# Small products of a chunk regrouped by row count on TensorE, and the decays' product on all 128 rows

## The chip, the cores and the metric

The kernel runs on one core of one Trainium2 chip. The metric is the device time of one execution in microseconds (us), as the median over runs. Matrix products run on TensorE (PE in the profile, its weight loads PEld), elementwise work on VectorE (DVE) and ScalarE (ACT), small helpers and some DMA issues on GpSimd (POOL), most loads are issued from SyncE (SP).

## The reference, cut to what matters

One decoder layer is computed for a prompt of 2048 tokens and for a small group of sample tokens. First comes a mixer with two recurrent halves, then cross-attention to 256 memory tokens, then a gated feed-forward part. The change touches the two recurrences of the prompt's mixer:

```python
def gla step(s, inp):                       # per chunk, per head, key width 64, value width 128
    qt = qc * exp(b);  kt = kc * exp(-b)
    att = where(causal, einsum('bthk,bshk->bhts', qt, kt), 0)
    o = einsum('bhts,bshv->bthv', att, vc) + einsum('bthk,bhkv->bthv', qt, s)
    s = exp(bl) * s + einsum('bshk,bshv->bhkv', kc * exp(bl - b), vc)

def ssd step(s, inp):                       # per chunk, 8 heads
    lc = cumsum(dt * a_head)
    decay = exp(where(causal, lc[t] - lc[s], -inf))
    y = (cc . bc) * decay * dt @ x  +  (cc . s) * exp(lc)
    s = exp(ll) * s + (exp(ll - lc) * dt * x) @ bc
```

The sum `o` of the first step is one product over 128 positions of the chunk (attention times values) plus one over 64 key entries (queries times state). The decays of the second step are differences of `lc`, so a row of `lc` has to be spread over 128 partitions. The kernel uses chunks of 128 tokens.

## The kernel before, in words

The prompt is handled in four blocks of 512 tokens (`block(b)`, L471), each of four chunks of 128 tokens. A block first projects its tokens (`fm`, L491, and `tm`, L628: long runs of 128-row products into banks `acc`, each row of weights times activations done as three products of the rounded parts by the helper at L125 to L129). The recurrences are cut into pieces by generators and put beside these projections through the queue `side`: SSD chunks (L709 to L778) run beside the projection `tm(1)` and those that follow it, GLA chunks (L847 to L895) of block b beside the projections of block b+1; the last block's GLA chunks run beside `folds(1)` (L424 to L468), which makes weight products for the attention stage and stores them through GpSimd's DMA queue (`wvo`). Beside blocks 0 and 1 also run, from the queue `back`, the memory keys and values, `folds(0)` and `quad_sums` (L406), whose loads and stores (`fold`, `wX`) go through GpSimd's queue too. All engines run their instructions in the written order, as the framework's scheduler has laid it down; nothing is reordered at run time apart from what an engine's own queue does.

Two places matter here.

A GLA chunk's second part (L865) makes, for each of four heads h = 2j + par, `dst = attm . v` over 128 rows (L882) and adds `q . Sp` over the 64 rows `par*64 ...` (L883). The heads of one `par` share a bank, `po[par]`. Before these stand the four products into `pS` (L875: 128 rows, 64 columns of weights), after them the next projection's products. A float32 product appears as two PE instructions in the trace, a rounded float32 (`F32R`) one as one.

An SSD chunk's first part (L709) builds `R`, 16 rows that hold the two parts of `lc` of 8 heads, masked, on GpSimd (L713), and multiplies it by ones (L739: 16 rows, 512 columns, twice), so that each of 128 partitions gets the sums. VectorE makes the decay matrix `M` from that (L743). `R` has one buffer, and shares it with a temporary of the gates (L610), which ScalarE and VectorE use earlier in the block.

Of the kernel before, what the change touches and what calls it, by code (L numbers as in the profile page):

```python
# [37 lines left out]
def f(ap):  # L38
    return ap.bitcast(F32)
# [3 lines left out]
def hymba_kernel(ctx: ExitStack, tc: tile.TileContext, a: dict, o: dict, dbg: dict | None = None):  # L43
# [427 lines left out]
    def block(b):  # L471
# [129 lines left out]
        def gates():  # L601
            pss = []
            nc.scalar.activation(sps[0:16], sp[0:16], AF.Copy)
            nc.vector.tensor_tensor(sps[32:48], sp[0:16], f(sps)[0:16], op=ALU.subtract)
            nc.scalar.activation(sps[64:80], sp[0:16], AF.Copy)
            for j in range(2):
                ps = mxt()
                nc.tensor.matmul(ps, lhsT=w2s[:, j * P:(j + 1) * P], rhs=sps, start=True, stop=True)
                pss.append(ps)
            logsig(bb[:, 0:2], pss, pa.tile([P, 2, BT], F32, name="R"), BT)  # L610
            for j in range(2):
                nc.vector.tensor_tensor_scan(bb[:, j], rmask, bb[:, j], 0.0, op0=ALU.mult, op1=ALU.add)
            b3 = bb[:, 0:2].rearrange("p j (c t) -> p (j c) t", t=CH)
            e8 = lambda t: t.rearrange("p j c -> p (j c)")
            nc.scalar.activation(e8(em), b3[:, :, 63], AF.Exp, scale=1.0 / 16)
            nc.scalar.activation(e8(ebl), b3[:, :, CH - 1], AF.Exp, scale=1.0 / 16)
            nc.vector.tensor_tensor(e8(el), b3[:, :, CH - 1], b3[:, :, 63], op=ALU.subtract)
            nc.scalar.activation(el, el, AF.Exp, scale=1.0 / 16)
            nc.vector.tensor_tensor(bb[:, 2:4].rearrange("p j (c t) -> p (j c) t", t=CH), b3, b3[:, :, 63:64].broadcast_to([P, 2 * NCH, CH]), op=ALU.subtract)
            nc.scalar.activation(bb[:, 0:2], bb[:, 2:4], AF.Exp, scale=1.0 / 16)  # L620
            nc.scalar.activation(bb[:, 2:4], bb[:, 2:4], AF.Exp, scale=-1.0 / 16)
            yield

        side.append(decays())
        step(side)
        side.appendleft(gates())
# [82 lines left out]
        def ssd_first(c):  # L709
            cs = slice(c * CH, (c + 1) * CH)  # L710

            R = pa.tile([16, 8, CH], F32R, name="R")
            nc.gpsimd.tensor_tensor(out=R, in0=lcT[:, cs].unsqueeze(1).broadcast_to([16, 8, CH]),  # L713
                                    in1=bmask.unsqueeze(2).broadcast_to([16, 8, CH]), op=ALU.mult)
            M = pa.tile([P, 8, CH], F32, name="M")

# [19 lines left out]
                                    triu.unsqueeze(1).broadcast_to([P, 2, CH]), op=ALU.mult)  # L736
            for g in range(2):
                pl = mxt()
                nc.tensor.matmul(pl, lhsT=onesr[0:16, :], rhs=R[:, 4 * g:4 * g + 4], start=True, stop=True)  # L739
                plv = pl.rearrange("p (h t) -> p h t", t=CH)  # L740
                for h in range(4):
                    s1 = lc[:, c * 8 + 4 * g + h:c * 8 + 4 * g + h + 1]
# [122 lines left out]
        def gla_second(c, am, kt_):  # L865
# [5 lines left out]
            for j in range(2):  # L871
                for par in range(2):
                    r0 = par * 64
                    h = 2 * j + par
                    nc.tensor.matmul(pS[r0:r0 + 64, j * P:(j + 1) * P], lhsT=kt_[:, h * 64:(h + 1) * 64], rhs=v[c][:, h * P:(h + 1) * P], start=True, stop=True)  # L875
            po = [mxt(), mxt()]
            for par in range(2):
                for j in range(2):
                    r0 = par * 64
                    h = 2 * j + par  # L880
                    dst = po[par][:, j * CH:(j + 1) * CH]
                    nc.tensor.matmul(dst, lhsT=am[:, 2 * par + j], rhs=v[c][:, h * P:(h + 1) * P], start=True, stop=False)  # L882
                    nc.tensor.matmul(dst, lhsT=q[r0:r0 + 64, j, cs], rhs=Sp[r0:r0 + 64, j], start=False, stop=True)  # L883
            for j in range(2):
                nc.vector.tensor_scalar(Sg[:, j], Sg[:, j], ebl[:, j, c:c + 1], None, op0=ALU.mult)
                nc.vector.scalar_tensor_tensor(Sg[:, j], pS[:, j * P:(j + 1) * P], el[:, j, c:c + 1], Sg[:, j], op0=ALU.mult, op1=ALU.add)
            ss = small.tile([P, 8], F32, name="ss")
            of = lambda h: po[h % 2][:, (h // 2) * P:(h // 2 + 1) * P]
            for h in range(4):
                nc.scalar.activation(v[c][:, h * P:(h + 1) * P], of(h), AF.Square, accum_out=ss[:, h:h + 1])  # L890
            rs = rstd_of(ss[:, 0:4], "rs", 128, cols=4)
# [1348 lines left out]
```

## Time and profile before

| | |
|---|---|
| time, median of 3 runs | 3048.89 us (3040.87 to 3052.48) |
| the profiled execution's own time | 3045.82 us |
| its span, first to last instruction | 3044.1 us |
| PE busy (matmul) | 2884.3 us, 95% |
| DVE, ACT, POOL busy | 2087.5, 1525.7, 544.3 us |
| mean granted TensorE clock | 0.977 |
| the four blocks with their recurrences | the first 914 us |

The page's times are us unless marked ns. A row of the timeline gives the start, the length, engine, line, operation, tiles, shape (rows*columns of the weights, then the moving operand) and how many instructions were merged; in brackets stands the engine's idle time before it and what ended it. Matmuls are pipelined, so a matmul's length is longer than its share of the time: the pitch from one start to the next is what it costs. The chain of waits goes back from the end, at each step to what released the instruction. A window's row gives, for each engine, busy time and instructions, then the granted TensorE clock and the DMA share.

### The profile page before, as it was taken

The numbers are of one execution on the slowest core, as the hardware profiler recorded it, in microseconds if no ns is written. First come the engines' busy times: TensorE is split into PE (matmuls) and PEld (weight loads), VectorE is DVE, ScalarE is ACT, GpSimd is POOL, SyncE is SP. The second block draws the span as 40 slices with busy tenths as digits, with TensorE's granted clock in tenths as the row PEclk, the third lists the DMA queues.
The fourth block names the chain that finished last, engine by engine and source line by source line (L and its number), as shares of the span: only waits on it lengthen the run. The fifth ranks groups of instructions, "written<-read, shape, count | busy, mean of one in ns | idle before, by whom it ended". The sixth has DMA issues, their size and how long they took to land.

```text
span 3044.1 us, 42288 instructions
## 1 busy us (share of the span) xinstructions
PE 2884.3 (95%) x15207; PEld 2408.6 (79%) x15207; DVE 2087.5 (69%) x3915; ACT 1525.7 (50%) x3044; POOL 544.3 (18%) x749
## 2 busy tenths in 40 slices
PE   8999999999997999999689999999999998999997
PEld 8887777787775778877588888888999995587875
DVE  7666676666737677677587777776678884566576
ACT  4454443554445677776554434433455553444453
POOL 2142341121321321024222100010000000011122
PEclk9999999999999999999799999999999999999998
DMA  7345543242256676467646455774243345767788
GB/s 239 118 152 161 169 125 118 70 128 75 78 187 226 242 263 227 153 202 237 195 177 212 163 172 186 258 265 160 101 150 121 119 141 183 245 139 192 158 210 246
DMA packets 154769, 529.89 MB, mean 174 GB/s; under 512 B 19360, under 2 KB 22608, under 8 KB 143040
## 3 DMA queue, kind: packets, MB, share of 16 engines
q1 hardware_dynamic: 93168, 331.75, 34.1%
q0 software_dynamic: 49152, 170.46, 18.4%
q10 hardware_dynamic: 12240, 24.99, 2.5%
q8 instruction: 120, 1.97, 0.3%
q14 instruction: 89, 0.73, 0.1%
HBM read 373.04 MB, written 154.09 MB: 173 GB/s over the span
## 4 chain that ended last, share of the span: by engine, by line
PE 57%; issue 16%; DMA 7%; DVE 6%; ACT 5%; POOL 2%; POOLq 0%; DVEq 0%; ACTq 0%; SPq 0%
PE accA L127 7%; PE accA L128 7%; PE accA L129 7%; PE accC L127 4%; PE acc L127 4%; PE acc L128 4%; PE acc L129 4%; PE accC L128 4%; PE accC L129 4%; PE accB L127 2%; PE accB L128 2%; PE accB L129 2%; PE mx L1911 1%; PE mx L1686 1%; DMA st<-wT 1%
## 5 line engine op out<-in xcount | busy, mean ns | idle before, releaser
L127 PE MATMUL accA<-r,s 128*128 128x512 f32 (+2 forms) x1792 | 645.3, 360 | 39.0 <-ACT r L1566 13.4
L129 PE MATMUL accA<-r,s 128*128 128x512 f32 (+2 forms) x1792 | 633.6, 354 | 7.1 <-DVE s L1504 6.2
L128 PE MATMUL accA<-r,s 128*128 128x512 f32 (+2 forms) x1792 | 633.9, 354 | 6.7 <-DVE r L1570 6.6
L127 PEld LDWEIGHTS accA<-r,s 128*128 128x128 f32 x1792 | 341.7, 191 | 114.7 <-ACT r L1566 17.5
L1502 ACT ACTIVATE s<-sum 128x512 fp32r<-128x512 f32 (+2 forms) x488 | 289.3, 593 | 268.4 <-DVE sum L1484 102.7
L128 PEld LDWEIGHTS accA<-r,s 128*128 128x128 f32 x1792 | 342.3, 191 | 40.8 <-DVE r L1570 12.0
L129 PEld LDWEIGHTS accA<-r,s 128*128 128x128 f32 x1792 | 341.9, 191 | 38.7 <-DVE s L1504 9.0
L127 PE MATMUL accC<-r,s 128*128 128x512 f32 (+2 forms) x896 | 325.3, 363 | 17.1 <-ACT r L1566 6.8
L1504 DVE TENSOR_TENSOR s<-sum,s 128x512 fp32r<-128x512 f32 (+2 forms) x488 | 308.8, 641 | 35.2 <-ACT s L1502 31.9
L129 PE MATMUL accC<-r,s 128*128 128x512 f32 (+2 forms) x896 | 317.9, 355 | 7.0 <-DVE s L1504 7.0
L128 PE MATMUL accC<-r,s 128*128 128x512 f32 (+2 forms) x896 | 317.6, 354 | 1.0 <-DVE r L1570 0.9
L1504 DVE TENSOR_TENSOR s<-raw,s 128x512 fp32r<-128x512 f32 (+2 forms) x366 | 234.3, 640 | 59.1 <-ACT s L1502 57.6
L1502 ACT ACTIVATE s<-raw 128x512 fp32r<-128x512 f32 (+2 forms) x366 | 218.2, 596 | 54.1 <-PE accC L129 51.3
L121 ACT ACTIVATE whi<-wraw 128x1024 fp32r<-128x1024 f32 (+2 forms) x148 | 137.1, 941 | 211.3 <-PE acc L128 107.2
L127 PEld LDWEIGHTS accC<-r,s 128*128 128x128 f32 x896 | 172.0, 192 | 61.4 <-issue 10.2
L122 DVE TENSOR_TENSOR wlo<-wraw,whi 128x1024 fp32r<-128x1024 f32 (+2 forms) x148 | 166.8, 1136 | 63.4 <-ACT whi L121 62.7
L129 PEld LDWEIGHTS accC<-r,s 128*128 128x128 f32 x896 | 171.8, 192 | 24.7 <-DVE s L1504 8.7
L1570 DVE TENSOR_TENSOR r<-st,r 128x1024 fp32r<-128x1024 f32 (+2 forms) x133 | 136.5, 1028 | 75.1 <-ACT r L1566 74.5
L128 PEld LDWEIGHTS accC<-r,s 128*128 128x128 f32 x896 | 172.0, 192 | 17.1 <-DVE r L1570 2.4
L127 PE MATMUL acc<-xh,whi 128*128 128x512 f32 (+1 forms) x464 | 170.1, 368 | 8.4 <-ACT xh L282 8.2
L129 PE MATMUL acc<-xh,wlo 128*128 128x512 f32 (+1 forms) x464 | 165.3, 358 | 1.7 <-DVE wlo L122 1.7
L128 PE MATMUL acc<-xl,whi 128*128 128x512 f32 (+1 forms) x464 | 164.7, 356 | 0.2 <-DVE xl L283 0.2
(643 smaller groups left out, 5765.0 us busy)
## 6 DMA issues: line engine op xcount, KB each, us to landing
raw<-in_w_gu_dram SPq DMA_DIRECT2D x66, 1024.0 KB, 4.9
wraw<-in_w_in_fm_dram SPq DMA_DIRECT2D x52, 512.0 KB, 3.7
wraw<-in_w_in_tm_dram SPq DMA_DIRECT2D x48, 512.0 KB, 3.7
yp<-y POOLq DMA_DIRECT2D x48, 512.0 KB, 6.9
raw<-aT SPq DMA_DIRECT2D x24, 768.0 KB, 5.3
st<-in_w_down_dram SPq DMA_DIRECT2D x34, 512.0 KB, 6.8
aT<-og POOLq DMA_DIRECT2D x22, 768.0 KB, 4.3
hX<-y POOLq DMA_DIRECT2D x32, 512.0 KB, 5.1
```

Of the source, the lines that this page charges most:

```text
L121: last[0] = nc.scalar.activation(hi[:, cs], raw[:, cs], AF.Copy)
L122: nc.vector.tensor_tensor(lo[:, cs], raw[:, cs], f(hi)[:, cs], op=ALU.subtract)
L127: nc.tensor.matmul(ps, lhsT=wh, rhs=ah, start=start, stop=False, skip_group_check=more)
L128: nc.tensor.matmul(ps, lhsT=wh, rhs=al, start=False, stop=False, skip_group_check=more)
L129: nc.tensor.matmul(ps, lhsT=wl, rhs=ah, start=False, stop=stop, skip_group_check=more)
L1502: nc.scalar.activation(h3, v, AF.Copy)
L1504: return lambda: nc.vector.tensor_tensor(l3, v, f(h3), op=ALU.subtract)
L1570: nc.vector.tensor_tensor(lo, v, f(hi), op=ALU.subtract)
L1686: nc.tensor.transpose(ps[kt // 4][:, kt % 4 * P:(kt % 4 + 1) * P], u[:, kt * P:(kt + 1) * P], ident)
L1911: nc.tensor.matmul(ps[g0:g0 + 32], lhsT=s_f[:, kt].rearrange("p h t -> p (h t)"), rhs=ws.popleft(), start=kt < 4, stop=kt >= FT - 4, tile_ ...
```

## The change

In a GLA chunk the four `attm . v` products come first, in a row, and then the four `q . Sp` products, whose heads now alternate between rows 0 to 63 and 64 to 127. Only the first `attm . v` product of each bank has the start flag. In an SSD chunk `R` becomes a tile of 128 rows, allocated once per block at the end of the gates and cleared there by GpSimd; the masked `lc` is written to rows 0 to 15 of it, and the product with ones takes all 128 rows.

```diff
@@ gates()
             nc.scalar.activation(bb[:, 2:4], bb[:, 2:4], AF.Exp, scale=-1.0 / 16)
+            Rs.append(pa.tile([P, 8, CH], F32R, name="R"))
+            nc.gpsimd.memset(f(Rs[0]), 0.0)
             yield
+        Rs = []
@@ ssd_first(c)
-            R = pa.tile([16, 8, CH], F32R, name="R")
-            nc.gpsimd.tensor_tensor(out=R, in0=lcT[:, cs].unsqueeze(1).broadcast_to([16, 8, CH]),
+            R = Rs[0]
+            nc.gpsimd.tensor_tensor(out=R[0:16], in0=lcT[:, cs].unsqueeze(1).broadcast_to([16, 8, CH]),
                                     in1=bmask.unsqueeze(2).broadcast_to([16, 8, CH]), op=ALU.mult)
...
-                nc.tensor.matmul(pl, lhsT=onesr[0:16, :], rhs=R[:, 4 * g:4 * g + 4], start=True, stop=True)
+                nc.tensor.matmul(pl, lhsT=onesr, rhs=R[:, 4 * g:4 * g + 4], start=True, stop=True)
@@ gla_second(c, am, kt_)
             po = [mxt(), mxt()]
+            of = lambda h: po[h % 2][:, (h // 2) * P:(h // 2 + 1) * P]
+
             for par in range(2):
                 for j in range(2):
-                    r0 = par * 64
                     h = 2 * j + par
-                    dst = po[par][:, j * CH:(j + 1) * CH]
-                    nc.tensor.matmul(dst, lhsT=am[:, 2 * par + j], rhs=v[c][:, h * P:(h + 1) * P], start=True, stop=False)
-                    nc.tensor.matmul(dst, lhsT=q[r0:r0 + 64, j, cs], rhs=Sp[r0:r0 + 64, j], start=False, stop=True)
+                    nc.tensor.matmul(of(h), lhsT=am[:, 2 * par + j], rhs=v[c][:, h * P:(h + 1) * P], start=j == 0, stop=False, skip_group_check=True)
+            for h in range(4):
+                r0, j = (h % 2) * 64, h // 2
+                nc.tensor.matmul(of(h), lhsT=q[r0:r0 + 64, j, cs], rhs=Sp[r0:r0 + 64, j], start=False, stop=True, skip_group_check=True)
```

On PE, in the first GLA chunk (in block 1, between `pS` and the next projection), the order before:

```order
L129 MATMUL acc<-xh_2912,wlo 128x512
L875 MATMUL mx<-v_2687,kt__2930 64x128 x4
L882 MATMUL mx<-v_2687,attm_1688 128x128
L883 MATMUL mx<-Sp,q 128x128
L882 MATMUL mx<-v_2687,attm_1688 128x128
L883 MATMUL mx<-Sp,q 128x128
```

(two more such pairs follow, then L127), and in the changed kernel, where L879 is the old L875, L886 the old L882 and L889 the old L883:

```order
L129 MATMUL acc<-xh_2910,wlo 128x512
L879 MATMUL mx<-v_2685,kt__2928 64x128 x4
L886 MATMUL mx<-v_2685,attm_1690 128x128 x4
L889 MATMUL mx<-Sp,q 128x128 x4
L127 MATMUL acc<-xh_2867,whi 128x512
L128 MATMUL acc<-xl_2868,whi 128x512
```

The eight products keep their place among PE's other work; they change places among themselves, and so do those of the other 15 chunks.

On GpSimd, at the start of block 2's SSD chunks (`carry` and `pre` belong to the convolution of the projection before them, `xw` is the SSD chunk's weighted input), the changed kernel has

```order
L534 COPY pre<-carry 128x3
L537 COPY carry<-pre 128x3
L534 COPY pre<-carry 128x3
L623 MEMSET R 128x1024
L717 TENSOR_TENSOR R<-lcT,bmask 16x1024
L729 TENSOR_TENSOR xw<-xdt,wl__5252 128x512
L717 TENSOR_TENSOR R<-lcT,bmask 16x1024
```

The clearing of `R` is the only new row there, ahead of the block's first write of `R` (before: L713); the rows around it stand as they did. The decays' products themselves (L739 before, L743 now) keep their places: this is PE around one of block 2's SSD chunks, before, and the changed kernel reads the same with the new line numbers:

```order
L733 MATMUL mx<-xc 128x128 x2
L739 MATMUL mx<-R,onesr 128x512
L127 MATMUL acc<-xh_4609,whi 128x512
L128 MATMUL acc<-xl_4610,whi 128x512
L129 MATMUL acc<-xh_4609,wlo 128x512
L739 MATMUL mx<-R,onesr 128x512
L127 MATMUL acc<-xh_4614,whi 128x512
L128 MATMUL acc<-xl_4615,whi 128x512
```

Nothing moved here: only the number of rows that L739 reads is another.

Of the 32 decays' products, 10 stand in five pairs, two in a row, and 22 stand alone among the projections' products or next to L733. Outside these places one product of `folds(1)` in the last block's tail stands a few rows earlier; nothing else moved.

More of the change, by code (lines that the diff above doesn't have):

```diff
@@ L887, in gla_second @@
             ss = small.tile([P, 8], F32, name="ss")
-            of = lambda h: po[h % 2][:, (h // 2) * P:(h // 2 + 1) * P]
             for h in range(4):
```

## The prediction

> **What bounds the kernel now.** First the page's busy times, then a table of windows over the blocks' part of the span (window and length, busy us and instructions of PE, PEld, DVE, ACT, POOL, then granted clock, DMA share, GB/s):
>
> ```profile
> PE 2884.3 (95%) x15207; PEld 2408.6 (79%) x15207; DVE 2087.5 (69%) x3915; ACT 1525.7 (50%) x3044; POOL 544.3 (18%) x749
> 130.00:302.40 172.40, 170.62 (x1010) 137.92 (x1010) 116.81 (x202) 81.55 (x156) 55.88 (x60) 1.00 0.48 150
> 302.40:387.60 85.20, 74.87 (x354) 58.19 (x352) 52.14 (x124) 42.71 (x67) 32.70 (x54) 0.98 0.50 159
> 387.60:459.00 71.40, 66.34 (x315) 53.25 (x316) 53.88 (x98) 29.88 (x58) 34.43 (x34) 0.94 0.44 129
> 459.00:866.00 407.00, 402.55 (x1951) 319.80 (x1949) 256.35 (x508) 181.90 (x338) 76.74 (x79) 0.99 0.32 95
> 873.00:904.00 31.00, 30.47 (x162) 22.28 (x162) 15.95 (x40) 17.94 (x42) 13.18 (x20) 1.00 0.65 216
> ```
>
> PE is busy nearly throughout, except in 302 to 459 (most of block 1). Busy PE is not yet the path, so the chain of waits was read window by window: the shares in 462 to 866 (blocks 2 and 3), in 302.3 to 387.7, and three long pieces of the chain.
>
> ```profile
> by line: PE acc L127 20.7%; PE acc L128 20.0%; PE acc L129 20.0%; PE mx L882 3.3%; PE mx L883 3.3%; PE mx L757 3.1%; ACT xc L198 1.8%; PE acc L516 1.8%; PE mx L767 1.8%; PE mx L694 1.8%; PE mx L754 1.7%; PE mx L739 1.6%; issue 1.6%; PE mx L
> by line: DMA fold<-in_w_out_dram 32.1%; issue 21.0%; DMA wX<-fold 17.6%; DMA wqk<-fold 6.0%; POOL fold L413 3.9%; DVE fraw L419 3.8%; DVE xc L541 3.6%; POOL wX L421 3.1%; DVE fold L419 2.9%; DVE wlo L122 2.6%; POOL R L713 2.2%; DVE sp L550
> 302.39 5.14 DMA wqk<-fold
> 879.43 5.50 DMA wvo<-fold
> 903.87 0.44 PE mx L860 x2
> ```
>
> In blocks 2 and 3 the chain is PE itself: L882 and L883 hold 6.6% of it, L739 1.6%. From 302.39 to 387.6 it is the round of loads and stores in `quad_sums` (`fold`, `wX`) on GpSimd's queue, and PE waits on its effects. In the tail it runs from 873 over the stores of `wvo` and comes back to PE only at 903.87, though PE is busy for 30.47 of 31.00 us: there both are about level.
>
> **The GLA products.** This is PE's timeline at the first chunk, and the group of L882 over the run:
>
> ```profile
> 273.90 0.66 PE L875 MATMUL mx<-v,kt__2930 128*64 128x128 f32 x8
> 274.49 0.49 PE L882 MATMUL mx<-v,attm 128*128 128x128 f32 x2
> 274.91 0.48 PE L883 MATMUL mx<-Sp,q 64*128 64x128 f32 x2
> 275.32 0.49 PE L882 MATMUL mx<-v,attm 128*128 128x128 f32 x2
> ...
> 277.82 0.50 PE L127 MATMUL acc<-xh,whi 128*128 128x512 f32 x1
> L882 PE MATMUL mx<-v,attm 128*128 128x128 f32 x128 | 31.3, 326 | 0.0
> ```
>
> Sixteen instructions take 277.82 - 274.49 = 3.33 us, and each product (two instructions) 0.42 us. The group counts 128, which is 16 chunks of 8, and shows no wait before any of them. Products of one kind in a row are much cheaper, as other rows show (128 rows first, then L854, which has the shape of L883 on both halves):
>
> ```profile
> 619.26 0.61 PE L733 MATMUL mx<-xc 128*128 128x128 f32 x4
> 619.80 0.49 PE L739 MATMUL mx<-R,onesr 16*128 16x512 f32 x1
> 644.86 1.89 PE L757 MATMUL mx<-xdt,M 128*128 128x64 f32 x16
> 646.59 1.08 PE L767 MATMUL mx<-xw,Bt 128*128 128x256 f32 x4
> 283.57 0.72 PE L854 MATMUL mx<-q,k 64*128 64x128 f32 x8
> 284.22 0.44 PE L860 MATMUL mx<-ident,k 128*128 128x128 f32 x2
> ```
>
> L757's sixteen start 1.73 / 16 = 0.108 us apart. L733's four take 0.54 us to the start of the 16-row product; with 0.21 of that for the step between row counts (half of the 0.42), the three inner steps are 0.11 each. L854's eight, four per half, take 0.65 us to the next kind, less than eight such steps: the halves run beside each other. So a chunk becomes 0.42 (the first product, with its entry and the step out) + 6 x 0.11 = 1.08 for the 128-row ones, and 0.65 for the 64-row ones: 1.73 instead of 3.33, a saving of 1.6 us, 25.6 in 16 chunks. The ends are that nothing improves (0), and that the steps between kinds vanish too: 8 x 0.11 and 4 x 0.11 with the halves beside each other, 1.3 us, a saving of 2.0 (32 over the run). I take 1.6: shape, halves and the two banks are those of L854, and L854 does pay a step in and out.
>
> What is queued behind: the third `attm . v` product waits for the second mask on VectorE, and it now comes 1.0 us earlier (0.65 instead of 1.67 after the first). No row of the group waits now (0.0); were a mask late by that much, 1.0 of the 1.6 us would go. L883's operand `Sp` is used later than before. ScalarE's squares (L890) need whole banks; bank 0 was full after 1.67 us, and is now at about 1.7; bank 1 at 1.7 instead of 3.33. Nothing after them is later.
>
> **The decays' products.** One alone, one after another, and the group:
>
> ```profile
> 620.56 0.40 PE L128 MATMUL acc<-xl,whi 128*128 128x512 f32 x1
> 620.79 0.40 PE L129 MATMUL acc<-xh,wlo 128*128 128x512 f32 x1
> 621.12 0.50 PE L739 MATMUL mx<-R,onesr 16*128 16x512 f32 x1
> 621.55 0.50 PE L127 MATMUL acc<-xh,whi 128*128 128x512 f32 x1
> 621.88 0.39 PE L128 MATMUL acc<-xl,whi 128*128 128x512 f32 x1
> 637.20 0.73 PE L739 MATMUL mx<-R,onesr 16*128 16x512 f32 x2
> 638.20 0.39 PE L128 MATMUL acc<-xl,whi 128*128 128x512 f32 x1
> L739 PE MATMUL mx<-R,onesr 16*128 16x512 f32 x32 | 14.8, 481 | 6.3 <-POOL R L713 5.5 <-ACT Bt L730 0.4 <-DVE s_z L661 0.3
> ```
>
> From L129 at 620.79 over L739 to L128 at 621.88 three starts take 1.09 us; the projection's own pitch is 0.23 (620.56 to 620.79), so as 128-row products they take 0.69, and 0.40 is saved. In a pair, L739 to L128 takes 1.00 against 3 x 0.23 = 0.69, and 0.1 before it (0.21 for the step in, against 0.11): again 0.40, for two. With 22 alone and 5 pairs, 27 x 0.40 = 10.8 us. A product of zeros costs no more than one of 128 rows, since the pitch of 0.23 is that of 128 full rows with the same 512 columns.
>
> **The clearing and the waits around R.**
>
> ```profile
> L682 POOL MEMSET attm<- 128x512 f32 x2 | 1.0, 545 | 0.0
> 583.63 1.89 POOL L713 TENSOR_TENSOR R<-lcT,bmask 16x1024 fp32r<-16x1024 f32 x1 [26.86 <-ACT z L666]
> ```
>
> Four clearings of twice that width cost about 1.1 us each on GpSimd. In block 2 they fall into the 26.86 us in which GpSimd waits anyway; without that cover, block 2's first L739 would be 1.1 us later, four times 4.4 in all. The first write of `R` no longer waits for ScalarE, only for `lcT` and the clearing: a few tenths once or twice, counted as nothing. In block 1 the clearing stands among `quad_sums`' stores, and those next in the queue could go 1.1 us later; its range is 0 to 1.1.
>
> **What of it reaches the end.** PE's saving is 25.6 + 10.8 = 36.4 us. It arrives where PE is the chain, and is lost where PE only comes sooner to something else's end. Two such waits in block 1, and four of the chunks:
>
> ```profile
> 325.18 0.44 PE L860 MATMUL mx<-ident,k 128*128 128x128 f32 x2 [1.83 <-DVE gt L894]
> 343.75 1.01 PE L694 MATMUL mx<-ident,gt 128*128 128x128 f32 x4 [2.45 <-DVE gt L894]
> 313.55 0.49 PE L882 MATMUL mx<-v,attm 128*128 128x128 f32 x2
> 332.11 0.49 PE L882 MATMUL mx<-v,attm 128*128 128x128 f32 x2
> 882.04 0.49 PE L882 MATMUL mx<-v,attm 128*128 128x128 f32 x2
> 896.70 0.49 PE L882 MATMUL mx<-v,attm 128*128 128x128 f32 x2
> ```
>
> The rows of L882 are the first of four chunks. Those at 313.55 and 332.11 each stand before one of these two waits, within the `quad_sums` chain that began at 302.39: their 3.2 us become longer waits. The first two chunks come before 302.39 and move its start. In the tail those at 882.04 and 896.70 lie in the `wvo` chain from 873 to 903.87; I count them lost as well, another 3.2, since that chain has no slack to give. The tail's first chunk and its last, before 873 and after 904, count. So 12 x 1.6 = 19.2 remain. Of the decays' products, blocks 2 and 3 hold 7 places each (6 alone, one pair), 2.8 us each, less 0.1 for one that stands behind a wait: 5.4. Of block 0's 2.4 and block 1's 2.8 I count about 1.8 and 1.4, because the first ones there stand behind waits (5.5 us on `R` in three waits, above) and `quad_sums` goes on to 438. That is 8.6.
>
> 19.2 + 8.6 = 27.8. The profiled execution took 3045.8 us, span 3044.1 and 1.7 around it, so 3018.0; the median of the runs lies 3.1 above it, which gives **3021 us**.
>
> **Rivals.** *All of it arrives*: block 1 and the tail follow PE after all. 36.4 less: 3012.5. For: PE is busy 30.47 of 31.00 us in the tail. Against: the chain in 302 to 387 is DMA by more than half.
>
> *Weight loads don't overlap*: if, in a run of 128-row products, each had to load its weights after the one before, they would go at the present 0.21 us, not at 0.11; a chunk would take 0.42 + 6 x 0.21 + 0.65 = 2.33, and save 1.0; 12 + 8.6 = 20.6, 3028. L733 and L757 speak against it. The Trainium skill ("TensorE: Matmul & The Clock Gate", Part 3, The mechanism) says that a weight load overlaps running products only when its row group is another, by which this rival should be the rule; the trace's 0.108 us for 128-row products disagrees.
>
> *It doesn't do what it says*: the 0.42 per product comes from adding into a bank just written, not from the row counts, and stays. Then only the decays' part is left: 8.6, 3040. L875 and L739 have steps of the same size without adding to anything, which is against it.
>
> *Swallowed*: with PE faster, block 0 and parts of blocks 2 and 3 turn out to be bound by VectorE (256.35 of 407 us busy) or loads, and half arrives: 14, 3035.
>
> *Slower*: idle stretches of PE cost clock.
>
> ```profile
> 344.95:348.35 3.40, 3.40 (x10) 2.62 (x9) 2.20 (x5) 0.54 (x1) 1.51 (x3) 0.50 0.52 190
> ```
>
> After the wait that ended at 343.75 the granted clock is 0.50 for 3.4 us, a loss of 1.7. If waits in 302 to 459 and 873 to 914 grow by the time saved before them, each may cost one or two such stretches more. With ten waits and two each that is 34 us, against 18 saved in blocks 2 and 3 (8 x 1.6 + 5.4): 3065. It decides from some 11 stretches on (18 / 1.7). The Trainium skill ("TensorE: Matmul & The Clock Gate", Part 1) gives the same halving after an idle window of about 3.4 us. Against it: inside the DMA-bound stretches a slower PE is itself hidden by the chain.
>
> **How the numbers follow.** Chances: forecast 0.58, all arrives 0.10, weight loads 0.08, swallowed 0.12, doesn't do it 0.07, slower 0.05. The likeliest's own range, from waits and the clock's stretches (a few of 1.7 us each way) and from the runs' spread, is 3012 to 3030; the range reaches to 3037 for part of "swallowed", and to 3008 below. A measurement of this kernel can tell 0.5%, 15 us, from no change: below 3033.6 is faster, which the forecast, the first two rivals and a third of "swallowed" give, 0.80. "Doesn't do it" and the rest of "swallowed" are same, 0.15; slower 0.05.
>
> **What would show it.** L882's successor in groups of 8 from first to last start within 0.9 us, and 1.7 us from its first start to the next projection product; 64-row instructions starting in twos; the decays' product as a 128-row one at a pitch of 0.23; blocks 2 and 3 shorter by 18 us together; the waits at 325 and 344 longer by 1.6 each. If PE's work shrinks so and the span doesn't follow by at least 20, the sum over the chain is wrong; if a chunk stays over 2.3 us, the price is.

## The result, and the profile after

| | median (lowest to highest) | ratio to before, 95% interval |
|---|---|---|
| before | 3049.85 us (3040.87 to 3052.48) | |
| after | 3013.75 us (3010.56 to 3020.39) | 0.989 [0.9863, 0.9916] |

The change takes 36.1 us off the median, 1.2%. The forecast was 3021 us, within 3008 to 3037. The profiled execution took 3010.56 us, span 3008.8; before it was 3045.82 and 3044.1. PE's busy time went from 2884.3 to

```profile
PE 2842.5 (94%) x15207; PEld 2385.9 (79%) x15207; DVE 2086.4 (69%) x3915; ACT 1523.9 (51%) x3044; POOL 551.9 (18%) x753
```

with the other engines about as they were. To see where the time went, the span is cut at places that both kernels have: the first `attm . v` product of each block's first GLA chunk, and the first product of the attention stage (tile `accA`). The windows between them, first before (block 2's stretch, block 3's, and the tail), then after; columns as in the prediction:

```profile
492.24:684.21 191.97, 189.61 (x929) 150.48 (x927) 125.42 (x252) 89.98 (x169) 39.07 (x41) 0.99 0.32 95
684.21:868.67 184.46, 182.37 (x900) 144.72 (x899) 114.00 (x231) 80.02 (x151) 37.67 (x38) 1.00 0.29 87
868.67:918.02 49.35, 43.29 (x228) 31.57 (x227) 20.92 (x56) 25.12 (x66) 15.83 (x24) 0.97 0.66 225
```

```profile
481.00:662.47 181.47, 179.41 (x928) 145.64 (x926) 124.90 (x252) 89.51 (x169) 41.27 (x42) 1.00 0.34 101
662.47:838.34 175.87, 173.78 (x900) 141.01 (x898) 113.42 (x231) 79.57 (x151) 39.23 (x39) 1.00 0.31 92
838.34:886.13 47.79, 38.58 (x229) 29.12 (x227) 20.88 (x56) 24.72 (x66) 15.88 (x24) 0.93 0.67 232
```

Blocks 2 and 3 became shorter by 10.5 and 8.6 us, as much as PE's busy time in them (10.2 and 8.6). In the tail PE is busy for 4.7 us less, but only 1.6 of it reached the end, and the granted clock fell from 0.97 to 0.93. The same cuts for all profiles of this study, in us, with the forecast's saving by stage in the last row (GLA products and decays' products together):

| profile | to the first chunk | block 1 | block 2 | block 3 | tail | the rest |
|---|---|---|---|---|---|---|
| before | 274.5 | 217.8 | 192.0 | 184.5 | 49.3 | 2126.1 |
| before, again (e3) | 274.6 | 218.4 | 191.9 | 184.5 | 48.9 | 2126.0 |
| after | 271.8 | 209.2 | 181.5 | 175.9 | 47.8 | 2122.7 |
| after, again (e5) | 274.9 | 204.7 | 181.5 | 175.8 | 48.2 | 2130.3 |
| GLA alone (e1) | 273.5 | 208.5 | 184.0 | 178.1 | 48.9 | 2129.0 |
| decays alone (e2) | 272.3 | 215.7 | 187.9 | 182.2 | 50.3 | 2127.8 |
| pairs on 128 rows (e4) | 273.8 | 208.0 | 184.4 | 178.3 | 45.6 | 2122.2 |
| half by half (e6, e10) | 271.7, 274.5 | 210.1, 208.5 | 181.5, 181.6 | 175.9, 175.9 | 45.5, 45.6 | 2132.2, 2131.8 |
| more fold buffers (e7) | 272.1 | 209.8 | 181.5 | 175.8 | 43.0 | 2129.7 |
| `quad_sums` from SP (e8) | 273.4 | 203.1 | 181.4 | 175.8 | 45.0 | 2126.4 |
| both (e9) | 275.4 | 199.9 | 181.5 | 175.8 | 42.8 | 2127.5 |
| forecast saving | 1.8 | 4.6 | 9.1 | 9.1 | 3.2 | 0 |

Blocks 2 and 3 repeat within 0.1 us, and block 1 of the changed kernel (after, e5, e6, e10, e7) spreads over 5.4. The first and the last stage move by 3.7 and 10 us from one profile to the next with no relation to the change. So of the 35.3 us between the two profiled spans, 6.1 (2.7 before the first chunk, 3.4 after the tail) can't be credited to it; 29.2 arose in between. Between the two repeats (e3 and e5) the same stages give 33.5.

**The price of a chunk.** PE's timeline at the first chunk of the changed kernel (start, length, then what ran):

```profile
271.24 0.66 PE L879 MATMUL mx<-v,kt__2928 128*64 128x128 f32 x8
271.82 1.16 PE L886 MATMUL mx<-v,attm 128*128 128x128 f32 x8
272.91 0.71 PE L889 MATMUL mx<-Sp,q 64*128 64x128 f32 x8
273.56 0.50 PE L127 MATMUL acc<-xh,whi 128*128 128x512 f32 x1
```

273.56 - 271.82 = 1.74 us from the first `attm . v` to the next projection product, where it was 3.33. Inside, the eight 128-row starts lie 0, 0.21 and then 0.11 us apart, the step out is 0.21, and the 64-row starts come in twos, 6 ns apart in a two and 0.10 to 0.11 between the twos, with 0.21 after the first two. So each change of the row count slows two starts from 0.11 to 0.21 us, which is 0.2 us in all; in the kernel before, the row count changes with every product, and all sixteen starts lie 0.20 to 0.21 apart. No row of either group waited for anything, nor did L743 wait for more than before (the two GLA groups, and the decays'; after the bar busy us, mean ns, idle before):

```profile
L886 PE MATMUL mx<-v,attm 128*128 128x128 f32 x128 | 18.5, 288 | 0.0
L889 PE MATMUL mx<-Sp,q 64*128 64x128 f32 x128 | 11.4, 297 | 0.0
L743 PE MATMUL mx<-R,onesr 128*128 128x512 f32 x32 | 14.4, 470 | 5.2 <-POOL R L717 3.7 <-ACT Bt L734 1.3 <-DVE s_z L665 0.2
```

### The profile page after: what moved, and what is told of

Same layout as the page of the kernel before. It is cut to its first block, busy times and chain, and to the rows that moved or that the text cites. A ratio compares the mean times of both kernels' runs of the same rounds, so it can differ in the third digit from the quotient of the medians.

```text
span 3008.8 us, 42293 instructions
## 1 busy us (share of the span) xinstructions
PE 2842.5 (94%) x15207; PEld 2385.9 (79%) x15207; DVE 2086.4 (69%) x3915; ACT 1523.9 (51%) x3044; POOL 551.9 (18%) x753
## 4 chain that ended last, share of the span: by engine, by line
PE 56%; issue 16%; DMA 7%; DVE 6%; ACT 5%; POOL 2%; POOLq 0%; DVEq 0%; ACTq 0%; SPq 0%
PE accA L127 7%; PE accA L128 7%; PE accA L129 7%; PE accC L127 4%; PE acc L127 4%; PE accC L128 4%; PE accC L129 4%; PE acc L128 4%; PE acc L129 4%; PE accB L127 2%; PE accB L128 2%; PE accB L129 2%; PE mx L1916 1%; PE mx L1691 1%; ACT r L1571 1%
## 5 line engine op out<-in xcount | busy, mean ns | idle before, releaser
L127 PE MATMUL accA<-r,s 128*128 128x512 f32 (+2 forms) x1792 | 643.5, 359 | 39.5 <-ACT r L1571 13.5
L129 PE MATMUL accA<-r,s 128*128 128x512 f32 (+2 forms) x1792 | 631.7, 353 | 7.7 <-DVE s L1509 7.0
L127 PEld LDWEIGHTS accA<-r,s 128*128 128x128 f32 x1792 | 340.5, 190 | 115.8 <-ACT r L1571 18.1
L129 PEld LDWEIGHTS accA<-r,s 128*128 128x128 f32 x1792 | 340.7, 190 | 39.2 <-DVE s L1509 9.6
L127 PE MATMUL accC<-r,s 128*128 128x512 f32 (+2 forms) x896 | 324.9, 363 | 18.7 <-ACT r L1571 6.8
L129 PE MATMUL accC<-r,s 128*128 128x512 f32 (+2 forms) x896 | 317.8, 355 | 7.4 <-DVE s L1509 7.4
L1507 ACT ACTIVATE s<-raw 128x512 fp32r<-128x512 f32 (+2 forms) x366 | 218.2, 596 | 53.2 <-PE accC L129 50.9
L127 PEld LDWEIGHTS accC<-r,s 128*128 128x128 f32 x896 | 171.5, 191 | 63.0 <-issue 11.2
L129 PEld LDWEIGHTS accC<-r,s 128*128 128x128 f32 x896 | 171.7, 192 | 25.1 <-DVE s L1509 9.1
L127 PE MATMUL acc<-xh,whi 128*128 128x512 f32 (+1 forms) x464 | 168.3, 364 | 8.4 <-ACT xh L282 8.3
L135 POOL TENSOR_TENSOR rs<-ms,nhalf 128x1 f32<-128x1 f32 (+4 forms) x125 | 105.8, 848 | 329.2 <-DVE ms L133 322.1
L129 PE MATMUL acc<-xh,wlo 128*128 128x512 f32 (+1 forms) x464 | 164.2, 355 | 1.7 <-DVE wlo L122 1.7
```

What stands on the lines that cost most here:

```text
L127: nc.tensor.matmul(ps, lhsT=wh, rhs=ah, start=start, stop=False, skip_group_check=more)
L129: nc.tensor.matmul(ps, lhsT=wl, rhs=ah, start=False, stop=stop, skip_group_check=more)
L135: nc.gpsimd.tensor_tensor(out=rs[:rows, :cols], in0=ms[:rows, :cols], in1=nhalf[:rows, :cols], op=ALU.pow)
L1507: nc.scalar.activation(h3, v, AF.Copy)
```

## The experiments

Ten runs followed, on three occasions, each time with runs of the kernel before beside them. Line numbers are those of the changed kernel unless said otherwise.

### The parts alone, and the kernel before once more (e1, e2, e3)

e1 takes the decays' part out of the change, so that only the GLA products are regrouped; e2 takes the regrouping out; e3 is the kernel before, unchanged.

```diff
e1:
-            R = Rs[0]
-            nc.gpsimd.tensor_tensor(out=R[0:16], ...
+            R = pa.tile([16, 8, CH], F32R, name="R")
+            nc.gpsimd.tensor_tensor(out=R, ...
-                nc.tensor.matmul(pl, lhsT=onesr, ...
+                nc.tensor.matmul(pl, lhsT=onesr[0:16, :], ...
e2:
-                    nc.tensor.matmul(of(h), lhsT=am[...], ...)
-            for h in range(4):
-                nc.tensor.matmul(of(h), lhsT=q[r0:r0 + 64, j, cs], ...)
+                    nc.tensor.matmul(dst, lhsT=am[...], ...)
+                    nc.tensor.matmul(dst, lhsT=q[r0:r0 + 64, j, cs], ...)
```

> Only the GLA products are regrouped; R stays a tile of 16 rows with its product on 16 rows. Theory of the prediction, corrected by the trace after (steps between row counts cost PE time, and what PE saves arrives where PE is the chain): each of the 16 chunks takes 1.73 us from its first product to the next projection's, blocks 2 and 3 are 6.4 us shorter each, block 1 gains 3 to 6, the tail 1.5 to 3: 18 to 22 us less than before. Rival, that the two halves of the change need each other (block 1's and the tail's other chains swallow it when PE is slower elsewhere): 12.8 of blocks 2 and 3 only, 13 us.

> Only the decays' product is on all 128 rows; the GLA products alternate as before, 3.33 us a chunk. By the sum of the prediction 8.6 us less than before (PE saves 0.40 at each of 27 places, 10.8). From the trace after: 2.2 to 4.1 in block 2 and block 3 each, about 1 in block 0, 0 to 2.8 in block 1: 6 to 10 us. Rival, that a product on 16 rows costs nothing beyond its own columns: 0 us, and the clearing of R in GpSimd's queue could make it 1 us slower.

> The kernel before, profiled once more, nothing changed. The comparison of before and after showed 1.95 us of the difference ahead of anything that was changed (at 13 to 18 us) and 3.4 us after 918, and quicker landings of wqk<-fold and wX<-fold at 302 to 322. If these are chance between two executions, this trace differs from the first one by amounts of that size at those places, and by nothing in blocks 2 and 3. If they come from the change, this trace agrees with the first one there within 0.5 us.

Measured, beside before at 3047.41 us: e1 3024.38 us, ratio 0.9926 [0.9914, 0.9939]; e2 3038.47 us, 0.9967 [0.9954, 0.998]; e3, a single run, 3045.94 us. So the GLA part alone saves 23.0 and the decays' part 8.9, together 31.9; the whole change saved 36.1 against its own runs of before and 29.1 in e5. The parts add up within that spread.

e1 saved 1 us more than its 18 to 22: block 1 gave 9.3 where 3 to 6 were expected, the tail 0.4 where 1.5 to 3 were. e2 lies in its range. e3 agrees with the first profile of before in the first stage (274.6) and in the rest (2126.0), and in the landings of `wqk` and `wX` that it names (5.2 and 4.6 us). By its own expectation that puts all of these differences down to the change. e5, the changed kernel again, has 274.9 and 2130.3 us in those two stages, so they are chance all the same; the landings are taken up below.

The windows of blocks 2 and 3, of e1 and then of e2:

```profile
482.00:666.00 184.00, 181.65 (x929) 145.84 (x927) 125.14 (x252) 89.52 (x169) 40.26 (x41) 1.00 0.34 99
666.00:844.00 178.00, 175.92 (x900) 141.14 (x898) 113.70 (x231) 79.51 (x151) 38.26 (x38) 1.00 0.30 91
```

```profile
488.00:675.90 187.90, 185.84 (x929) 149.14 (x927) 125.23 (x252) 89.92 (x169) 39.99 (x42) 1.00 0.32 97
675.90:858.10 182.20, 180.12 (x900) 144.48 (x898) 113.75 (x231) 79.95 (x151) 38.57 (x39) 1.00 0.29 88
```

Block 3: 6.4 less in e1 (to the first decimal, four chunks of 1.6), 2.3 less in e2, 8.6 with both. The decays' part of block 3 can be read place by place, from the starts of PE's rows in before and in e2: its four chunks save 0.57, 0.68, 0.66 and, for the pair, 0.28 us, 2.2 in all. Block 2: 8.0 less in e1 and 4.1 in e2, and 10.5 with both, not 12.1. The excess of 1.6 to 1.8 in each is one thing that is counted once. In the kernel before, a stretch of half clock lies in this block, at the same place in both of its profiles (the second row is e3's), and after has none (third fence):

```profile
587.30:590.70 3.40, 3.40 (x10) 2.62 (x9) 2.73 (x6) 1.06 (x1) 1.64 (x1) 0.50 0.00 0
```

```profile
588.10:591.50 3.40, 3.40 (x10) 2.62 (x9) 2.73 (x6) 1.06 (x1) 1.64 (x1) 0.50 0.00 0
```

```profile
567.60:571.00 3.40, 3.35 (x15) 2.75 (x16) 2.81 (x9) 1.91 (x4) 2.89 (x2) 1.00 0.02 5
```

3.4 us at half clock are 1.7 us. None of the profiles with a part of the change has a stretch there. So block 2's 10.5 are 6.4 + 2.3 + 1.7, to within 0.1. In before, PE waits for 1.16 us shortly ahead of the stretch (the L739 at 585.57); e1 has the same wait, and no stretch after it. Its length alone doesn't decide; what else may is in the last section.

### Which property of the pairs costs the time (e4, e6, e10)

e4 leaves the order of the kernel before as it was, pairs that alternate and add into the bank just written, and lets the second product of each pair take all 128 rows. Each head then gets the state's share of both heads of its pair, so e4 computes another output and stands for the time alone. e6 keeps the regrouping and runs the 64-row products one half after the other; e10 is e6's kernel, run several times.

```diff
e4 (on the kernel before):
-                    nc.tensor.matmul(dst, lhsT=q[r0:r0 + 64, j, cs], rhs=Sp[r0:r0 + 64, j], start=False, stop=True)
+                    nc.tensor.matmul(dst, lhsT=q[:, j, cs], rhs=Sp[:, j], start=False, stop=True)
e6, e10 (on the changed kernel):
-            for h in range(4):
+            for h in (0, 2, 1, 3):
```

> The order of before, attm.v and q.Sp in turn, adding into the same bank, but q.Sp takes all 128 rows (the query and state rows of both heads of a pair: the output is another, since each head gets the state's share of both). Theory, that 0.42 us per product comes from the step between row counts: the 16 instructions go at 0.11 us and a chunk takes 1.8 to 2.1 us. Rival, that it comes from adding into a bank just written: it stays at 3.33 us. Rival, that a change of the weights' operand (attm, then q) costs it: stays at 3.33 too.

> The changed kernel, but the four q.Sp products are issued half by half: heads 0 and 2 (rows 0 to 63), then 1 and 3 (rows 64 to 127). Theory of the prediction, from L854 whose products are issued in that order too: each half has a queue of its own, instructions of the two halves start in twos, and a chunk stays at 1.73 us. Rival, that the alternation is what lets them run side by side: the eight go one after another, 8 x 0.11 and the step out instead of 0.65, and a chunk takes 2.1 to 2.2 us.

> The kernel of e6 once more, timed. It differs from the changed kernel in the order of the heads (no change of a chunk's time, 1.74 us) and in one product of folds(1), which stands in the tail where it stood before the change. Theory, that this place decides over the tail: 45.5 us again, and no half-clock stretch at 872, against 47.8 and 48.2 in two executions of the changed kernel. Rival, chance: 47 to 48. In all 3010 to 3020, not to be told from the changed kernel.

Measured: e4 3013.93 us, e6 3018.54 (one run each); e10 3018.53 us, 0.9907 [0.989, 0.9924]. PE's timeline at e4's first chunk (two more pairs in the gap), and at e6's:

```profile
273.79 0.49 PE L882 MATMUL mx<-v,attm 128*128 128x128 f32 x2
274.12 0.39 PE L883 MATMUL mx<-Sp,q 128*128 128x128 f32 x2
274.34 0.39 PE L882 MATMUL mx<-v,attm 128*128 128x128 f32 x2
...
275.60 0.48 PE L127 MATMUL acc<-xh,whi 128*128 128x512 f32 x1
```

```profile
271.67 1.16 PE L886 MATMUL mx<-v,attm 128*128 128x128 f32 x8
272.76 0.72 PE L889 MATMUL mx<-Sp,q 64*128 64x128 f32 x8
273.41 0.50 PE L127 MATMUL acc<-xh,whi 128*128 128x512 f32 x1
```

In e4 all sixteen instructions together take 1.81 us, 0.11 each, though they alternate between two operands and add into the same bank at once. So the 0.42 us per product of the kernel before came from the steps between row counts; the rivals in which the adding or the change of operand costs it are out. In e6 the chunk takes 1.74 us, as with alternating halves, and the instructions still start in twos, 14 ns apart. The halves run beside each other whichever order they are written in; of the two parts of the regrouping only the first, 128 rows apart from 64, bought time.

### The tail: buffers of the stores (e7)

In the tail, `folds(1)` copies each result with ScalarE into one of two buffers `fold`, from which GpSimd's queue stores `wvo`. e7 gives the first of each pair of results (`mt` = 0) two other buffers that are free by then.

```diff
-                t = pa2.tile([P, 512], F32, name="fold", bufs=2)
+                t = pa2.tile([P, 512], F32, name="fold", bufs=2) if mt else pa.tile([P, 512], F32, name=("xw", "xD")[n])
```

> The changed kernel, with four buffers instead of two for the results that folds(1) stores as wvo (two SSD buffers, idle by then, join the two of fold). Theory, that in the tail PE's saving is lost since ScalarE's copies wait for the landing of wvo stores from two buffers: the stretch from the first q.Sp chunk of the tail to the first accA product, 49.4 us before and 47.8 after, comes down to 43 to 45, and the whole is 3 to 4 us shorter. Rival, that the tail goes by GpSimd's queue (rs behind issues that wait for copies) and the squares on ScalarE: 47 to 48, no change.

Measured: 3012.72 us, 0.9887 [0.9861, 0.9914], beside before at 3045.0; e5, the changed kernel itself on the same occasion, 3015.89, 0.9897 [0.9876, 0.9919]. What ScalarE's copies (L453) waited for between 850 and 870 us, in after and in e7 (us, times):

```profile
  DMA wvo<-fold: 7.7, 4
```

```profile
  PE acc L129: 2.9, 4
```

The windows of the tail, e10's (which has the same order of PE's products there as e7) and e7's:

```profile
840.50:886.00 45.50, 37.31 (x228) 28.25 (x226) 20.98 (x56) 24.72 (x66) 15.85 (x24) 0.95 0.71 243
```

```profile
839.20:882.20 43.00, 36.49 (x228) 28.02 (x226) 20.87 (x56) 24.93 (x66) 15.82 (x24) 0.97 0.75 258
```

With the copies released from the stores the tail is 2.5 us shorter, and PE's waits at L864 go from 1.2 us in all to 0.5. e9, below, has the same buffers and the same order of products, and a tail of 42.8. That the landing of the stores held the tail is shown. The medians of e7 and e5 differ by 3.2 us, and their intervals overlap; only the stage shows it.

The other half of the tail is settled only in part. After, e5 and e1 have one product of `folds(1)` a few rows earlier than before, and their tails are 47.8, 48.2 and 48.9; e4, e6 and e10 have it where it was, with chunks as cheap, and theirs are 45.5 and 45.6. In after, PE waits in front of L864, and a stretch of half clock follows (PE's row, and the window; then the stretch in e5):

```profile
871.51 0.44 PE L864 MATMUL mx<-ident,k 128*128 128x128 f32 x2 [1.99 <-DVE gt L899]
```

```profile
872.94:876.35 3.41, 3.41 (x10) 2.61 (x9) 0.00 (x0) 0.72 (x2) 0.54 (x1) 0.50 0.36 136
```

```profile
871.59:875.00 3.41, 3.41 (x9) 2.58 (x9) 0.00 (x0) 0.58 (x1) 0.54 (x1) 0.50 0.27 102
```

PE is busy all through it, so 1.7 us are lost there. e1 has the same stretch (at 879.14), after a wait of 2.12 us; so all three of the longer tails have it. e8, below, has the product in the early place too and waits 1.8 us at L864, but has no such stretch, and its tail is 45.0. The early place alone is therefore not the cause. The stretch accounts for 1.7 of the 2 to 4 us by which the three are longer than e4, e6, e10 and e8; for the rest, 46.1 to 47.2 against 45.0 to 45.6, the record shows no cause.

### Block 1: the queue of `quad_sums` (e8, e5, e9)

e8 issues the loads and stores of `quad_sums` from SyncE's queue. e5 is the changed kernel once more, and e9 has e7's and e8's edits together.

```diff
-                    nc.gpsimd.dma_start(out=r.rearrange("p (k c) -> p k c", k=2), ...
+                    nc.sync.dma_start(out=r.rearrange("p (k c) -> p k c", k=2), ...
...
-                    nc.gpsimd.dma_start(out=wX[i, q][:, u, c], in_=t[at])
+                    nc.sync.dma_start(out=wX[i, q][:, u, c], in_=t[at])
```

> The changed kernel once more, as the mark for the other three on the same chip: 3010 to 3020 us, some 33 less than before. Theory that block 1's gain is no chance: the stores wqk<-fold and wX<-fold that took 5.1 and 5.0 us to land in three traces with chunks of 3.33 us, and 2.6 and 2.2 in three with chunks of 1.73 to 1.81, take 2.6 and 2.2 again. Rival, chance: they take 4 to 5 us in this execution.

> The changed kernel, with the loads and stores of quad_sums issued from SyncE's queue instead of GpSimd's. Theory, that block 1 is still held by GpSimd's queue, where rs and R stand behind issues that wait for landings: the 4.0 us wait of L698 at 334 and that on R at 379 go, and block 1 is 3 to 6 us shorter than in the changed kernel. Rival, that SyncE's queue then holds the projections' weight loads back behind the same waits: new waits on wraw, block 1 0 to 10 us longer.

> The changed kernel with both repairs, quad_sums' loads and stores from SyncE's queue and four buffers for the wvo stores. Theory that they add (they act in block 1 and in the tail): block 1 (first GLA chunk of block 0 to that of block 1) at 203 us as with the first alone, tail at 43 as with the second alone, 7 to 9 us less than the changed kernel up to the attention stage, 3005 to 3010 in all. Rival, that the tail's gain was one product's place in PE's order and not the buffers: tail at 45 to 46, as with quad_sums on SyncE's queue alone.

Measured: e5 as above; e8 3009.66 us, 0.9882 [0.9857, 0.9906]; e9 3006.44 us, 0.9871 [0.9851, 0.9891], beside before at 3046.54. e5 saved 29.1 us, where some 33 were expected. PE's waits for `gt` at L698 over 127 to 885 us (us in total, times, longest), in after, e8 and e9:

```profile
PE mx L698 <- DVE gt L899: 7.1, 2, 4.0
```

```profile
PE mx L698 <- DVE gt L899: 3.8, 2, 3.1
```

```profile
PE mx L698 <- DVE gt L899: 3.8, 2, 3.1
```

The wait of 3.1 is the tail's and stays; the one of 4.0 in block 1 falls to 0.7. The wait on `R`, which e8's expectation named too, stays (1.7 us, 2.0 in after). The first projection product behind the wait for `gt`, in after and in e8, shows what the queue was worth there:

```profile
335.15 0.78 PE L516 MATMUL acc<-xh,whi 128*128 128x512 f32 x1
```

```profile
333.43 0.48 PE L516 MATMUL acc<-xh,whi 128*128 128x512 f32 x1
```

Counted from the block's first chunk (at 271.82 and 273.45), that is after 63.3 us and 60.0 us. e9 has 60.0 as well, and the five profiles of kernels with after's `quad_sums` have 62.5 to 63.3. So up to this place the loads and stores on SyncE's queue gain 2.5 to 3.3 us.

Over the whole of block 1 the clock blurs this. The block takes 203.1 us in e8 and 199.9 in e9, against 204.7 to 210.1 in those five: e9 is below all five by at least 4.8, e8 below the best of them by 1.6 only (3 to 6 were expected of it, and 203 us of e9). But stretches of 3.4 us at half clock, up to 1.7 us lost in each, lie in this block six times in after (at 334, two in a row, 368, 402 and, two in a row, 446), four times in e5, three times in e8 and once in e9; before has five, e3 six. The granted clock over the block, after's and e9's rows:

```profile
271.80:481.00 209.20, 194.38 (x976) 157.67 (x974) 143.96 (x289) 98.97 (x183) 77.27 (x98) 0.95 0.50 153
```

```profile
275.40:475.30 199.90, 188.05 (x977) 152.09 (x975) 143.72 (x289) 99.87 (x183) 47.39 (x50) 0.99 0.52 161
```

With 1.7 us taken off for each stretch, e8 and e9 come to 198 us, and so do after, e5, e10 and e7 to within 2 (197.8 to 199.6; e6 201.6). Whether the other queue brought fewer such stretches, or chance did, no run separates. e9 is the fastest kernel of the study, 40 us below the runs of before beside it, where after was 29 and 36 below.

How the rounds of `quad_sums` themselves changed is seen in GpSimd's rows. The second load of one round and the first two of the next, in the kernel before, in e2 (whose GLA chunks are the old ones), and in after; in brackets the idle time before and what ended it:

```profile
307.82 0.74 POOL L413 DMA_DIRECT2D fold<-in_w_out_dram  x1 [3.78 <-DMA wqk<-fold]
321.59 1.45 POOL L413 DMA_DIRECT2D fold<-in_w_out_dram  x2 [3.84 <-DMA wX<-fold]
```

```profile
305.43 0.73 POOL L413 DMA_DIRECT2D fold<-in_w_out_dram  x1 [3.58 <-DMA wqk<-fold]
318.91 1.45 POOL L413 DMA_DIRECT2D fold<-in_w_out_dram  x2 [3.92 <-DMA wX<-fold]
```

```profile
299.40 0.74 POOL L413 DMA_DIRECT2D fold<-in_w_out_dram  x1 [0.60 <-DMA wqk<-fold]
308.91 1.45 POOL L413 DMA_DIRECT2D fold<-in_w_out_dram  x2
```

From the one to the other it takes 13.8 and 13.5 us with the old chunks and 9.5 with the new ones (9.4 in e5). The store of `wqk` ahead of it landed after 4.9 to 5.2 us in the three profiles with the old chunks (before, e3, e2), and after 2.6 to 2.7 in the seven with cheap ones and `quad_sums` on GpSimd's queue; the first store of `wX` after 4.6 to 5.1, and 2.2. Part of that is given back: the next round is 13.0 us in after, 9.9 before.

Counted from the first chunk, chunk 3 of block 0 starts after 57.6 us before, and after 50.9 us in after: 6.7 earlier, which is three chunks of 1.6 and the wait of 1.83 before L860 (old numbering), which vanished. From there the rounds keep pace: the third round begins 6.8 us earlier, the sixth 6.1. The fourth chunk's 1.6 us went into the wait at L698, 4.0 us instead of 2.45. The rest of the 8.6 (and of e5's 13.1 to 13.7) comes after 380 us, where the decays' products stand and the waits and the half-clock stretches vary most.

Why the stores land sooner isn't settled. Between the kernels the times differ at which they meet the weight loads that SyncE issues; that this overlap slows them would fit, and no run separates it.

## Why the prediction was right, and where not

**The GLA products: right.** 1.73 us was forecast, and measured in 14 of the 16 chunks (behind the other two, in the tail, the next product waits for ScalarE or VectorE); L733's and L757's pitch of 0.11 and L854's halves were the right rows to price it by, and the step of 0.21 between row counts was the right name for the cost (e4). All signs named for it came: the 128-row starts within 0.9 us, the 64-row ones in twos, 1.7 us in all, no late mask.

**Weight loads: the rival is out.** Successive instructions of the `attm . v` products have different weights of the same 128 rows, and start 0.11 us apart, while a load of 128 by 128 weights takes 0.19 (the row of PEld below). The Trainium skill ("TensorE: Matmul & The Clock Gate", Part 3, The mechanism) has loads overlap running products only for another row group; this trace disagrees again. On the step itself, the Trainium skill ("TensorEngine Tiling (Array Packing)", Tiling Modes, Key Properties) says that a change of tiling mode drains the engine, without a price; e4 against before agrees, with 1.81 us a chunk without the changes and 3.33 with them.

**The decays' products: the term of 0.40 us was too large.** Block 3 gained 2.3 in e2 where 2.7 to 2.8 were forecast. One alone in the changed kernel, and its weight load:

```profile
599.44 0.39 PE L128 MATMUL acc<-xl,whi 128*128 128x512 f32 x1
599.66 0.40 PE L129 MATMUL acc<-xh,wlo 128*128 128x512 f32 x1
599.93 0.47 PE L743 MATMUL mx<-R,onesr 128*128 128x512 f32 x1
600.24 0.39 PE L127 MATMUL acc<-xh,whi 128*128 128x512 f32 x1
600.47 0.40 PE L128 MATMUL acc<-xl,whi 128*128 128x512 f32 x1
```

```profile
599.90 0.19 PEld L743 LDWEIGHTS mx<-R,onesr 128*128 128x128 f32 x1 [0.27 <-issue]
```

From L129 to the second product after it (599.66 to 600.47) three starts take 0.81 us; the forecast had 0.69, before it was 1.09. So 0.28 is saved here, not 0.40; over block 3's seven places it is 2.2 us, 0.31 at each. The steps are 0.27 and 0.31 instead of 0.23, and the weight load starts only 0.03 us before its product, while in the same timeline the next projection product's starts at 600.01, 0.23 before its own. A semaphore instruction stands ahead of that load in PE's queue; that it makes the load late is argued, not isolated. The forecast priced the product as one more projection product, and those don't follow an instruction that waits.

**Blocks 2 and 3: 18 together forecast, 19.1 measured**, by two errors that offset each other: the decays' term, some 0.9 too large for both, and the 1.7 us of the half-clock stretch at 587 us, which the forecast didn't have. It counted the clock only as something to lose. A short stretch inside a stage that PE bounds can vanish as well as appear when the work ahead of it shifts.

**What is lost in block 1: wrong in size.** The forecast counted two chunks and half of the decays' products as lost to a `quad_sums` chain of fixed length from 302.39 us on, and 4.6 us as saved; 8.6 came in the first profile and 13.7 in the repeats, and 9 to 10 with the GLA part alone (e1). The chunk at 313.55 and the wait of 1.83 after it did arrive, since the round was shorter by 4 us: the chain's own pieces, the landings, did not keep their lengths. The step that failed is "their 3.2 us become longer waits". Of the two waits that should have grown by 1.6, that at 344 did (to 4.0), and that at 325 vanished.

**The tail: wrong in the other direction.** Four chunks make 6.4 us; 3.2 were forecast to arrive, 0.7 to 1.6 did. That chunks "lie in the `wvo` chain" named the right mechanism (e7), but it took more than two chunks: between 850 and 870 us ScalarE's copies waited 7.7 us for its stores, and 2.5 us came back when they didn't. Another 1.7 went with the half-clock stretch at 872.94. The last chunk, counted as arriving whole, gave 1.1 of its 1.6: behind it stands a wait of PE for `gt`, which grew from 2.6 us to 3.1 in every kernel with the regrouped products. It stays at 2.6 in e4, whose old order fills the first bank halfway through the chunk, so that ScalarE's squares can start on it; the regrouping fills both banks at the end. That this is the reason would fit and was not isolated.

**Block 0: the term of 1.8 us was too large.** The stage before the first chunk took 271.7 to 275.4 us over all profiles, with and without the change. Cut closer, from the block's first product with `R` to its first chunk, the four profiles with the old product take 123.6 to 124.1 us and the eight with the new one 122.5 to 124.8, on the mean 0.45 less. Two of the products with `R`, around 194 us, saved nothing there: the stretch around them takes 2.6 to 3.2 us with the old product and 2.7 to 3.1 with the new.

**The sum.** 27.8 us forecast, 36.1 and 29.1 between the medians of two comparisons, 29.2 and 33.5 in the stages that the change touches. Block 1 gave 4 to 9 more and block 2 1.4 more, the tail 2 less. The difference of 7 us to the measured median is about as large as what two executions of one kernel differ by in the first and the last stage. The slower rival had little to go on: one of the two waits did grow, and a half-clock stretch came in the tail, but block 2's went, and block 1 has six and four of them in the two profiles of the changed kernel against five and six in those of the kernel before.

## What to carry to other kernels

Where PE is the chain, sort small products by row count: a switch cost 0.2 us each way here, and a PE instruction of such a product 0.11. Price a regrouping by the pitch of a row that already runs in a row of its own kind, not by the length of one instruction, and price an instruction that waits for a semaphore a little above the pitch of those that don't. Where PE stands beside a chain of small loads and stores, don't take the chain's length as fixed; only the stages where PE itself is the chain repeat to 0.1 us, and there such a forecast is worth making.

## What was not expected of the hardware

The two halves of TensorE took their 64-row products as if each had its own queue: written half after half, the instructions still started 14 ns apart in twos, and the chunk took 1.74 us, against 1.73 with the halves in turn.

The product of the decays starts very soon after a float32 one in the changed kernel, as this row of PE's timeline shows:

```profile
598.85 0.28 PE L737 MATMUL mx<-xc 128*128 128x128 f32 x1
598.88 0.48 PE L743 MATMUL mx<-R,onesr 128*128 128x512 f32 x1
```

0.03 us lie between the two starts, less than the 0.11 between the float32 products ahead of them, and the next product comes 0.32 later; the two steps together are 0.35 us, about a float32 start and a projection product (0.11 + 0.23). In e4 the first projection product behind the float32 ones starts 0.03 us after the last of them too, so this seems to belong to the change from float32 to rounded float32 products, and not to the decays.

The same stores from the same queue, the last of `wqk` and the first of `wX`, landed in 2.2 to 2.7 us with cheap chunks ahead of them and in 4.6 to 5.2 with the old ones; later stores of `wX` in block 1 took anything between. From the second load of that round to the next round it took 13.5 to 13.9 us in the one case and 9.4 to 9.5 in the other (before, e3 and e2 against after and e5).

Within one execution all half-clock stretches start on one grid. Up to block 2 those of the kernel before start at 344.94, 389.31, 413.21, 457.58 and 587.29 us; the distances are 13, 7, 13 and 38 times 3.413 us, the length of one stretch. In every profile the starts fit such a grid, and it lies elsewhere in each. In after, e5 and e1 the wait of 2.0 to 2.1 us at L864 lies whole in the grid step just ahead of the stretch (in after between 869.53 and 872.94); in e8 a step ends at 864.57, in the middle of the wait of 1.8 us (863.78 to 865.56), and no stretch follows. It is the same with the wait of 1.16 us in block 2: whole in one step in before, cut in two at 568.53 in e1. So whether a stretch follows one of these waits seems to hang on where the grid happens to lie in that execution. It isn't the whole rule: in e6 and e10 waits of 1.3 and 1.2 us at L864 also lie whole in a step, and no stretch follows. This is read from these few cases; no run isolates it.
